# First layer's expert outputs kept as rows of a table that the second layer gathers, with half of each down weight split in two parts

## The chip, the cores and the metric

The kernel runs on one core of one Trainium2 chip. The metric is the device time of one execution in microseconds (us). Times named T+x are counted from one event of the profiled execution, which the text defines.

## What is computed

Two layers of a diffusion backbone over 512 latent tokens and 256 context tokens, width 1024, all float32. Each layer has an attention part and a mixture of experts; this is the mixture, cut to what matters here:

```python
# 16 experts in 4 groups; a token takes one group, and two experts inside it
for g in range(MOE_GROUPS):
    a = jnp.einsum('nd,edf->nef', h, w_gate[g])      # 1024 -> 256, per expert
    u = jnp.einsum('nd,edf->nef', h, w_up[g])        # 1024 -> 256
    hid = jax.nn.silu(a) * u * combine[:, g, :, None]   # zero but for the two chosen experts
    out = out + jnp.einsum('nef,efd->nd', hid, w_down[g])   # 256 -> 1024
...
x = x + mod_l[5] * f[:B * S].reshape(B, S, D)        # after layer 0: latent tokens
ctx = ctx + mod_c[5] * f[B * S:].reshape(ctx.shape)  # and context tokens
```

So a token's row after layer 0 is its row before, plus a gate row (one for latent, one for context tokens) times the sum of its two experts' outputs. Layer 1 norms that row first, and multiplies it with its input weights.

## The kernel before

Tokens stand in six tiles of 128 rows, taken in the order 4, 5 (context), 0, 1, 2, 3 (latent). Layer 0's output projection (`out_proj`) leaves the rows before the experts in DRAM as `F` and the normed rows as `H`, and the routing (`route_group`, `route`) gives each of the 16 experts up to 128 slots: `idx` holds the token of each slot.

**The expert loop** (`experts`, lines 1538 to 1594, called once per layer) runs over 16 experts, staggered: gate and up of expert e stand on TensorE ahead of down of expert e-1. Per expert:

- `fetch` (line 1026) gathers 128 rows of `H` through GpSimd's indirect DMA into `hg`; `expert_in` transposes them on TensorE and splits them in two float32r parts, `hh` on ScalarE and `hlo` on VectorE (`split`, lines 205 and 206).
- Weights come in units of 512 KB through `WeightStream`: four units with gate and up (two DMAs of 256 KB each), two with the down weight. 22 buffers hold them: the queue of SyncE issues a load when the buffer that it writes is free, in the order of use. Gate and up units are split in the parts `whi` and `wlo` as they come (`ahead`), at most four ahead (`nparts`), which frees the buffer; down units stay as they are until the matmuls have read them.
- `expert_up` (line 1043) multiplies in three terms of parts (hi hi, hi lo, lo hi), 24 matmuls of 512 columns into `eacc`. `expert_hid` transposes the hidden rows (`hidtr`) and copies them to `th`. `expert_down` (line 1079) does four plain float32 matmuls of 512 columns into two `yacc`; each stands in the profile as two instructions.
- `expert_gate` (line 1071) builds on VectorE the gate row of each slot (latent or context, by `ctx`), and `expert_down` multiplies `yacc` with it (line 1091) and adds the 128 rows to `F` by an indirect DMA with accumulation (line 1093), dropping empty slots:

```python
    nc.vector.tensor_tensor(y[:, cs], ya[n], gate[:, cs], op=ALU.mult)
i = nc.gpsimd.indirect_dma_start(F, bass.IndirectOffsetOnAxis(ap=idx[:, 1, x:x + 1], axis=0), y, None,
                                 compute_op=ALU.add, bounds_check=rows - 1, oob_is_err=False).ins
```

**The entry to layer 1** (in `emit`, lines 1633 to 1690) loads the six tiles of `F` (`xc`, three buffers, line 1665), and per tile `norm_hT` does: square and sum on ScalarE (line 779), reciprocal root on GpSimd (lines 211 and 212), scaling to `xn` on VectorE (line 781), eight transposes to `xtr` on TensorE, scale and shift to `tf` half on ScalarE and half on VectorE (lines 795 and 797), and the split into `hT` and `hL` (`hT1c` and `hL1c` for context tiles). Then TensorE multiplies with the key and value weights (`uk`, 256 columns) and, for latent tiles, with the first half of the query weights (`uq`, 512 columns, four units of two DMAs, loaded once the first `xc` has landed). TensorE's order in the expert loop is the program's (`manual_schedule`); at the entry the build's scheduler sets each engine's order. Every engine and queue works in order, so a waiting instruction holds what stands behind it.

## Time and profile before

| | us |
|---|---|
| median of 3 runs | 1223.6 (1219.67 to 1224.37) |
| the profiled execution | 1226.32, span 1224.6 |
| TensorE busy | 1105.9 (90%) |
| VectorE busy | 791.5 (65%) |
| ScalarE busy | 614.4 (50%) |
| GpSimd busy | 237.2 (19%) |

PE is TensorE's matmuls, PEld its weight loads, DVE VectorE, ACT ScalarE, POOL GpSimd, SP SyncE, and a name with q an engine's sequencer. A row of a timeline gives start, duration, engine, line, operation, output<-inputs, count, and in brackets how long the engine had been idle and what ended that. The expert loop of layer 0 lies at about 557 to 732 us, the entry to layer 1 at 732 to 800 us, the expert loop of layer 1 at 1043 to 1214 us.

### The profile page before, as it was taken

The numbers are of one execution on the slowest core, as the hardware profiler recorded it, in microseconds if no ns is written. First come the engines' busy times: TensorE is split into PE (matmuls) and PEld (weight loads), VectorE is DVE, ScalarE is ACT, GpSimd is POOL, SyncE is SP. The second block draws the span as 40 slices with busy tenths as digits, with TensorE's granted clock in tenths as the row PEclk, the third lists the DMA queues.
The fourth block names the chain that finished last, engine by engine and source line by source line (L and its number), as shares of the span: only waits on it lengthen the run. The fifth ranks groups of instructions, "written<-read, shape, count | busy, mean of one in ns | idle before, by whom it ended". The sixth has DMA issues, their size and how long they took to land.

```text
span 1224.6 us, 21495 instructions
## 1 busy us (share of the span) xinstructions
PE 1105.9 (90%) x7986; PEld 817.4 (67%) x7986; DVE 791.5 (65%) x1613; ACT 614.4 (50%) x1266; POOL 237.2 (19%) x252
## 2 busy tenths in 40 slices
PE   5999998998889989978999885989989996899996
PEld 2688887665556667866777654877766785677773
DVE  2532355677677753668888765677688447677773
ACT  3533644555466652216555536467588522555551
POOL 1000011224222000031222221331230004133321
PEclk8999999999899999978999996999999998899998
DMA  9711102776464428658999977012041374998992
GB/s 319 238 47 60 35 11 82 272 235 214 170 224 131 148 86 262 223 207 283 348 326 333 325 233 227 12 44 70 1 138 36 108 256 174 314 318 289 297 308 46
DMA packets 106251, 228.11 MB, mean 186 GB/s; under 512 B 21429, under 2 KB 30391, under 8 KB 106132
## 3 DMA queue, kind: packets, MB, share of 16 engines
q1 hardware_dynamic: 94324, 197.15, 48.0%
q0 software_dynamic: 9216, 22.09, 7.3%
q10 hardware_dynamic: 2592, 7.34, 1.5%
q8 instruction: 67, 1.10, 0.4%
q14 instruction: 52, 0.43, 0.1%
HBM read 210.60 MB, written 27.41 MB: 194 GB/s over the span
## 4 chain that ended last, share of the span: by engine, by line
PE 57%; DVE 8%; DMA 8%; ACT 4%; POOL 4%; issue 3%; SPq 1%; POOLq 0%; ACTq 0%; DVEq 0%
PE eacc L172 11%; PE acc L172 11%; PE yacc L172 7%; PE ptr L184 4%; DMA wraw<-in_exp_w_up_dram 4%; PE pv L172 4%; PE sc L172 4%; PE modps L172 3%; PE qacc L172 3%; PE hgtr L184 2%; PE co L172 2%; PE lg L172 2%; POOL rq L435 1%; DVE wlo L206 1%; PE h2tr L184 1%
## 5 line engine op out<-in xcount | busy, mean ns | idle before, releaser
L206 DVE TENSOR_TENSOR wlo<-wraw,whi 128x1024 fp32r<-128x1024 f32 (+2 forms) x184 | 210.2, 1156 | 80.9 <-ACT whi L205 71.0
L205 ACT CAST whi<-wraw 128x1024 fp32r<-128x1024 f32 (+2 forms) x184 | 181.1, 994 | 145.4 <-PE eacc L172 94.8
L172 PE MATMUL eacc<-whi,hh 128*128 128x512 f32 x256 | 119.7, 468 | 0.0
L172 PE MATMUL yacc<-wraw,th 128*128 128x512 f32 x256 | 115.2, 593 | 1.1 <-ACT th L1068 1.1
L172 PE MATMUL eacc<-whi,hlo 128*128 128x512 f32 x256 | 102.6, 401 | 0.0
L172 PE MATMUL eacc<-wlo,hh 128*128 128x512 f32 x256 | 102.2, 399 | 0.0
L172 PE MATMUL acc<-whi,hT 128*128 128x512 f32 (+2 forms) x256 | 91.8, 359 | 4.8 <-ACT hT L205 4.8
L172 PE MATMUL acc<-wlo,hT 128*128 128x512 f32 (+2 forms) x256 | 88.8, 347 | 0.5 <-DVE wlo L206 0.4
L184 PE MATMUL ptr<-cb,P 128*128 128x128 f32 x480 | 77.5, 284 | 12.8 <-ACT PT L540 6.4
L172 PE MATMUL acc<-whi,hL 128*128 128x512 f32 (+2 forms) x256 | 88.4, 345 | 0.0
L172 PEld LDWEIGHTS yacc<-wraw,th 128*128 128x128 f32 x256 | 48.2, 189 | 49.9 <-issue 44.1
L184 PEld LDWEIGHTS ptr<-cb,P 128*128 128x128 f32 x480 | 52.9, 141 | 38.8 <-ACT PT L540 9.9
L172 PE MATMUL modps<-mw,csT 128*32 128x512 f32 (+1 forms) x448 | 64.8, 571 | 10.4 <-DMA mw<-in_mod_w_dram 6.1
L172 PE MATMUL sc<-Kst,Qh 128*128 128x512 f32 (+2 forms) x192 | 64.7, 344 | 3.6 <-ACT P L544 3.5
L504 DVE CUSTOM_DVE_ANT_0 sc<-sc,mk,sink 128x512 f32<-128x512 f32 (+1 forms) x64 | 56.2, 882 | 16.8 <-PE sc L172 14.6
L540 ACT COPY PT<-ptr 128x512 f32<-128x512 f32 x96 | 56.1, 587 | 16.8 <-PE ptr L184 15.7
L172 PE MATMUL pv<-PT,z_k 128*64 128x256 f32 x480 | 63.7, 389 | 0.0
L172 PEld LDWEIGHTS eacc<-whi,hh 128*128 128x128 f32 x256 | 49.9, 195 | 14.5 <-issue 6.7
L172 PEld LDWEIGHTS eacc<-wlo,hh 128*128 128x128 f32 x256 | 50.0, 195 | 14.3 <-issue 6.7
L172 PEld LDWEIGHTS acc<-whi,hT 128*128 128x128 f32 x256 | 49.4, 193 | 14.5 <-ACT hT L205 5.2
L172 PE MATMUL sc<-Kst,Ql 128*128 128x512 f32 (+2 forms) x192 | 56.5, 316 | 1.1 <-DVE Ql L206 1.1
L172 PEld LDWEIGHTS eacc<-whi,hlo 128*128 128x128 f32 x256 | 49.3, 192 | 11.9 <-DVE hlo L206 0.7
(331 smaller groups left out, 2530.7 us busy)
## 6 DMA issues: line engine op xcount, KB each, us to landing
mw<-in_mod_w_dram SPq DMA_DIRECT2D x80, 512.0 KB
wraw<-in_exp_w_gate_dram SPq DMA_DIRECT2D x128, 256.0 KB
wraw<-in_exp_w_up_dram SPq DMA_DIRECT2D x128, 256.0 KB
wraw<-in_exp_w_down_dram SPq DMA_DIRECT2D x64, 512.0 KB
mw<-in_mod_w_dram SPq DMA_DIRECT2D x32, 256.0 KB
wraw<-in_ev_w_in_dram SPq DMA_DIRECT2D x12, 512.0 KB
wraw<-in_od_w_in_dram SPq DMA_DIRECT2D x20, 256.0 KB
wraw<-in_od_w_out_dram SPq DMA_DIRECT2D x16, 256.0 KB
```

The costliest lines, as they stand in the source:

```text
L172: return self.nc.tensor.matmul(out, lhsT=l, rhs=r, start=start, stop=stop)
L184: self.nc.tensor.transpose(out, in_, self.ident[:in_.shape[0], :in_.shape[0]])
L205: self.nc.scalar.copy(hi, src)
L206: self.nc.vector.tensor_tensor(lo, src, hi.bitcast(F32), op=ALU.subtract)
L435: nc.gpsimd.tensor_tensor(rq[:, 0, :], ms, self.mhalf[:, :8], op=ALU.pow)
L504: nc.vector.tensor_tensor_reduce(sc[:, lo:lo + L], sc[:, lo:lo + L], mask, rq[:, 1, h:h + 1], sink[:, 1, h:h + 1], ALU.add, ALU.min, mx[:, ...
L540: (nc.scalar.copy if a0 == 0 else nc.vector.tensor_copy)(u2["PT"][:, a0:a0 + m, j2, :], t[:, 0:m, :])
```

## The change

In layer 0 alone, an expert's output is no longer scaled and added to `F`: its 128 slots are copied from `yacc` (half by ScalarE, half by VectorE) and written as 128 rows of a DRAM table `Y` by a plain DMA from GpSimd's queue. The routing also computes for each token its two rows of the table (`slot`; one more row holds zeros, for a pair that got no slot). At the entry to layer 1, two indirect DMAs per tile gather these rows (`fetch_y`, two tiles ahead), and VectorE adds the two, multiplies with the gate row and adds to `xc`; latent tiles are written back to `F`. In layer 0 the first of the two down units of each expert is split in parts too, with one more unit ahead (`nparts` and the parts' buffers 5 in place of 4), and multiplies in three terms. Layer 1's expert loop stays.

```diff
-                    self.units.append((False, [(slice(0, 2), wd[...])]))
+                    self.units.append((l == 0 and q == 0, [(slice(0, 2), wd[...])]))
...
+            V.tensor_tensor(by, r["OH"], self.cst("iota")[:, None, None, 0:16].to_broadcast([P, 2, T, 16]), op=ALU.mult)
+            V.tensor_reduce(sl, by, axis=AX.X, op=ALU.add)
+            V.scalar_tensor_tensor(sl, sl, float(P), r["pos"], op0=ALU.mult, op1=ALU.add)
+            V.tensor_scalar(far, r["pos"], float(CAP), float(2 * NEXP * P), op0=ALU.is_ge, op1=ALU.mult)
+            V.tensor_tensor(sl, sl, far, op=ALU.add)
+            V.tensor_scalar(self.slot, sl, float(NEXP * P), None, op0=ALU.min)
...
-    def expert_gate(self, e, gate, isctx, wk):
-        y = wk.tile([P, D], F32, tag="y", name="y", bufs=2)
-        self.nc.vector.scalar_tensor_tensor(y, gate[1], isctx[:, e:e + 1], gate[0], op0=ALU.mult, op1=ALU.add)
...
+        hi, lo = [wk.tile([P, P], F32R, tag=n, name=n, bufs=2) for n in ("thh", "thl")]
+        self.split(hi, lo, t[:, 0, :])
+        self.nc.scalar.copy(th[:, 1, :], t[:, 1, :])
...
             for n in range(2):
-                self.mm(ya[n], h[:, q, :], w[:, n, :], q == 0, q == 1)
+                if not isinstance(w, tuple):
+                    self.mm(ya[n], (h[0] if isinstance(h, tuple) else h)[:, q, :], w[:, n, :], q == 0, q == 1)
+                    continue
+                for c, (a, b) in enumerate(((1, 0), (1, 1), (2, 0))):
+                    self.mm(ya[n], h[a], w[b][:, n, :], c == 0, False)
+        if gate is None:
+            for n in range(2):
+                (nc.scalar.copy, nc.vector.tensor_copy)[n](y[:, n * 512:(n + 1) * 512], ya[n])
+            nc.gpsimd.dma_start(self.Y[x * P:(x + 1) * P, :], y)
+            return
...
+        def fetch_y(t):
+            yi[t] = [spare(oh, 2 * (t % 2) + j) for j in range(2)]
+            return [nc.gpsimd.indirect_dma_start(yi[t][j], None, k.Y, bass.IndirectOffsetOnAxis(ap=k.slot[:, j, t:t + 1], axis=0)).ins
+                    for j in range(2)]
...
-            d = nc.sync.dma_start(xi[i], F[i * P:(i + 1) * P, :]).ins
+            ds = [nc.sync.dma_start(xi[i], F[i * P:(i + 1) * P, :]).ins]
+            if m not in g5:
+                g5[m] = spare(ol, m)
+                nc.sync.dma_start(g5[m], k.modD[0][m, 5 * D:6 * D].partition_broadcast(P))
+            if t < 2:
+                ds += fetch_y(t)
             if first is None:
-                first = d
+                first = ds[2]
...
+                ya, yb = yi[t]
+                nc.vector.tensor_tensor(ya, ya, yb, op=ALU.add)
+                nc.vector.tensor_tensor(ya, ya, g5[m], op=ALU.mult)
+                nc.vector.tensor_tensor(xi[i], xi[i], ya, op=ALU.add)
+                if t + 2 < 6:
+                    fetch_y(t + 2)
                 k.norm_hT(wk, pt, xi[i], AB1[:, m, :], k.modT[1][:, m, 0:8], *parts(i))
+                if i < 4:
+                    nc.scalar.dma_start(F[i * P:(i + 1) * P, :], xi[i])
```

Three places show what this does to the order of instructions. Each fence lists one engine's instructions in order (line, operation, output<-inputs, columns, count if repeated).

**TensorE, where down of one expert stands in layer 0's loop.** Before:

```order
L172 MATMUL eacc<-wlo,hh 128x512
L172 MATMUL eacc<-whi,hlo 128x512
L172 MATMUL yacc<-wraw,th 128x512 x4
L172 MATMUL eacc<-whi,hh 128x512
L172 MATMUL eacc<-wlo,hh 128x512
```

Now:

```order
L175 MATMUL eacc<-whi,hlo 128x512
L175 MATMUL yacc<-whi,thh 128x512
L175 MATMUL yacc<-wlo,thh 128x512
L175 MATMUL yacc<-whi,thl 128x512
L175 MATMUL yacc<-whi,thh 128x512
L175 MATMUL yacc<-wlo,thh 128x512
L175 MATMUL yacc<-whi,thl 128x512
L175 MATMUL yacc<-wraw,th 128x512 x2
L175 MATMUL eacc<-whi,hh 128x512
```

Two of the four float32 matmuls are now three matmuls of parts each; nothing else moved there.

**VectorE and ScalarE at the entry to layer 1, first tiles** (`wlo` and `whi` here are parts of the query weights `uq`). VectorE before:

```order
L781 TENSOR_SCALAR xn<-xc,ss 128x1024 x2
L797 TENSOR_SCALAR tf<-xtr,AB_4100,modT_70 128x128 x4
L781 TENSOR_SCALAR xn<-xc,ss 128x1024
L206 TENSOR_TENSOR hL1c<-tf,hT1c 128x4x128 x2
L781 TENSOR_SCALAR xn<-xc,ss 128x1024
L797 TENSOR_SCALAR tf<-xtr,AB_4100,modT_70 128x128 x2
L206 TENSOR_TENSOR wlo<-wraw,whi 128x1024
```

VectorE now, the first three rows and the next three being the adds of the first and the second tile:

```order
L1715 TENSOR_TENSOR early_oh_8053<-early_oh_8053 128x1024
L1716 TENSOR_TENSOR early_oh_8053<-early_oh_8053,early_ol_8054 128x1024
L1717 TENSOR_TENSOR xc<-xc,early_oh_8053 128x1024
L1715 TENSOR_TENSOR early_oh_8053<-early_oh_8053 128x1024
L1716 TENSOR_TENSOR early_oh_8053<-early_oh_8053,early_ol_8054 128x1024
L1717 TENSOR_TENSOR xc<-xc,early_oh_8053 128x1024
L209 TENSOR_TENSOR wlo<-wraw,whi 128x1024 x2
L786 TENSOR_SCALAR xn<-xc,ss 128x1024
L209 TENSOR_TENSOR wlo<-wraw,whi 128x1024 x2
L802 TENSOR_SCALAR tf<-xtr,AB_4102,modT_70 128x128 x4
L209 TENSOR_TENSOR hL1c<-tf,hT1c 128x4x128
```

ScalarE before:

```order
L779 ACTIVATE xn,ss<-xc 128x1024 x2
L795 ACTIVATE tf<-xtr,modT_70,AB_4100 128x128 x4
L779 ACTIVATE xn,ss<-xc 128x1024
L205 CAST hT1c<-tf 128x4x128 x2
L779 ACTIVATE xn,ss<-xc 128x1024
```

ScalarE now:

```order
L784 ACTIVATE xn,ss<-xc 128x1024
L208 CAST whi<-wraw 128x1024 x2
L784 ACTIVATE xn,ss<-xc 128x1024
L208 CAST whi<-wraw 128x1024 x2
L800 ACTIVATE tf<-xtr,modT_70,AB_4102 128x128 x4
L208 CAST hT1c<-tf 128x4x128 x2
```

The six adds and all four splits of `uq` now stand ahead of the first tile's `tf` on VectorE, and the four casts of `uq` ahead of it on ScalarE; before, the first split of `uq` stood behind the first tile.

**VectorE and GpSimd, between the first tile and the third one's `xn`** (the third tile, 0, is the first latent one). VectorE now, from the row behind the second tile's `xn` on:

```order
L209 TENSOR_TENSOR hL1c<-tf,hT1c 128x4x128
L1715 TENSOR_TENSOR early_oh_8053<-early_oh_8053 128x1024
L802 TENSOR_SCALAR tf<-xtr,AB_4102,modT_70 128x128 x4
L209 TENSOR_TENSOR hL1c<-tf,hT1c 128x4x128
L1716 TENSOR_TENSOR early_oh_8053<-early_oh_8053,early_ol_8054 128x1024
L209 TENSOR_TENSOR hL1c<-tf,hT1c 128x4x128
L1717 TENSOR_TENSOR xc<-xc,early_oh_8053 128x1024
L1715 TENSOR_TENSOR early_oh_8053<-early_oh_8053 128x1024
L405 TENSOR_REDUCE ms<-ktmp 128x2
L1716 TENSOR_TENSOR early_oh_8053<-early_oh_8053,early_ol_8054 128x1024
L1717 TENSOR_TENSOR xc<-xc,early_oh_8053 128x1024
L786 TENSOR_SCALAR xn<-xc,ss 128x1024
```

GpSimd now, around the reciprocal root (`ss`) of that third tile:

```order
L1688 DMA early_oh_8053<-Y,slot 128x1024 x2
L214 TENSOR_SCALAR ss<-ss 128x1
L1688 DMA early_oh_8053<-Y,slot 128x1024
L215 TENSOR_TENSOR ss<-ss,mhalf 128x1
L214 TENSOR_SCALAR ms<-ms 128x2
```

Before, the third tile's `xn` followed the first tile's `tf` directly, and no DMA stood in GpSimd's queue here. Now six adds (of the third and the fourth tile) stand between, and a gather for the sixth tile stands inside the root's pair; that gather needs the buffer that the fourth tile's adds read.

## Rows read from the trace of the kernel before

**Rows 1.** Busy time by stretch: stretch, its us, busy us and instructions, TensorE clock, DMA share, GB/s.

```profile
630.00:660.00 30.00, 30.00 (x127) 21.15 (x126) 25.89 (x30) 17.16 (x24) 7.87 (x6) 1.00 1.01 340
...
731.00:742.00 11.00, 0.00 (x0) 0.00 (x0) 0.57 (x1) 0.31 (x2) 1.56 (x1) 0.69 0.57 134
...
750.00:763.00 13.00, 10.26 (x66) 8.76 (x64) 10.51 (x19) 11.26 (x22) 3.09 (x6) 0.89 0.83 272
763.00:800.00 37.00, 37.00 (x217) 32.18 (x217) 24.68 (x60) 19.48 (x48) 12.52 (x18) 0.96 0.07 19
```

**Rows 2.** The chain that ended last: start us, us, what held it.

```profile
552.38 4.49 DMA hg<-H,idx
...
604.84 2.74 PE eacc L172 x12
607.58 3.43 PE yacc L172 x8
...
617.69 3.43 PE yacc L172 x8
...
688.24 10.28 DMA wraw<-in_exp_w_up_dram
...
703.43 3.43 PE yacc L172 x8
...
731.84 6.33 DMA F<-y,idx
738.25 3.43 DMA xc<-F
```

**Rows 3.** Timeline of ScalarE in layer 0's expert loop.

```profile
675.37 1.04 ACT L205 CAST whi<-wraw 128x1024 fp32r<-128x1024 f32 x1 [6.01 <-DMA wraw<-in_exp_w_up_dram]
```

**Rows 4.** DMA, 552 to 558 us, gathers alone: packets, MB, share of 16 engines.

```profile
q0 software_dynamic: 273, 1.01, 56.4%
```

**Rows 5.** DMA, 731 to 738 us, the last accumulation alone.

```profile
q0 software_dynamic: 272, 0.64, 56.1%
```

**Rows 6.** DMA, 597 to 698 us, by queue, and two kinds of issue.

```profile
q1 hardware_dynamic: 11663, 25.43, 68.6%
q0 software_dynamic: 2877, 7.84, 30.4%
...
F<-y,idx POOLq DMA_INDIRECT x10, 9.1
hg<-H,idx POOLq DMA_INDIRECT x9
```

**Rows 7.** Groups by line and shape, 571 to 735 us: count, busy us, mean ns.

```profile
L206 DVE TENSOR_TENSOR wlo<-wraw,whi 128x1024 fp32r<-128x1024 f32 x57 | 68.5, 1220 | 25.1 <-ACT whi L205 18.8 <-issue 4.1 <-DMA wraw<-in_exp_w_down_dram 0.8
L205 ACT CAST whi<-wraw 128x1024 fp32r<-128x1024 f32 x56 | 58.7, 1049 | 63.8 <-PE eacc L172 40.1 <-DMA wraw<-in_exp_w_up_dram 20.3 <-issue 2.4
...
L1091 DVE TENSOR_TENSOR y<-yacc,y 128x512 f32<-128x512 f32 x32 | 20.8, 681 | 1.6 <-PE yacc L172 1.4
L1076 DVE SCALAR_TENSOR_TENSOR y<-g,ctx,g 128x1024 f32<-128x1024 f32 x16 | 20.4, 1278 | 0.0
```

**Rows 8.** One line's instructions, `h<-h,B`: durations in ns, minimum, median, maximum.

```profile
L882 DVE TENSOR_TENSOR h<-h,B x6: 1212/1224/1226, 504.7 to 1022.7; 128x1024 f32<-128x1024 f32 x6
```

**Rows 9.** Timeline, from the last expert of layer 0 into layer 1.

```profile
730.88 0.69 DVE L1091 TENSOR_TENSOR y<-yacc,y 128x512 f32<-128x512 f32 x1 [0.17 <-PE yacc L172]
...
741.70 1.06 ACT L779 ACTIVATE xn<-xc 128x1024 f32<-128x1024 f32 x1 [10.69 <-DMA xc<-F]
...
744.02 0.75 DVE L781 TENSOR_SCALAR xn<-xc,ss 128x1024 f32<-128x1024 f32 x1
...
748.13 1.36 DVE L797 TENSOR_SCALAR tf<-xtr,AB,modT 128x128 f32<-128x128 f32 x4
...
750.59 0.56 PE L172 MATMUL acc<-whi,hT1c 128*128 128x256 f32 x1
...
751.03 12.92 SPq L317 DMA_DIRECT2D wraw<-in_od_w_in_dram  x11
```

66 lines of the change are left out of this document (39 added, 27 removed).

## The prediction

> **What bounds the kernel now.** I read the busy time by stretch first. In layer 0's expert loop TensorE is busy 30.00 of 30 us and the DMA engines are full at the same time (share 1.01, 340 GB/s); from 731 to 742 TensorE does nothing, and from 763 to 800 it is busy 37.00 of 37 us [rows 1]. So there are two places to look at: a loop with two limits, and an entry to layer 1 whose length is set by when TensorE gets its third tile, since after that it never waits.
>
> Next comes the chain that ended last. One expert takes 617.69 - 607.58 = 10.11 us, of which down (`yacc`) is 3.43 us, or 0.43 for each of its eight instructions, and twelve `eacc` take 2.74 us, 0.229 each [rows 2]. Late in the loop the chain leaves TensorE and runs through loads of weights, one of which lands 10.28 us after its issue, at 698.52 [rows 2]; the timeline shows ScalarE idle for 6.01 us until a weight has landed [rows 3]. From 607.58 to 703.43 nine experts took 95.85 us, 4.9 more than nine times 10.11 [rows 2]: that is what the loads cost the loop.
>
> At its end the last accumulation into `F` takes 6.33 us to land, then the first `xc` 3.43 [rows 2]. I count from T = 730.88 + 0.69 = 731.57, when VectorE has written the last output [rows 9]. Before, the first tile's square starts at 741.70 = T+10.1, its first product at 750.59 = T+19.0 [rows 9], and TensorE's unbroken work with the third tile at 763 = T+31.4 [rows 1].
>
> **TensorE in the loop.** Two of four float32 matmuls (four instructions of 0.43 = 1.72 us) become six matmuls of parts (6 x 0.229 = 1.37) [rows 2]: 0.34 us less per expert, 5.5 for sixteen, as long as nothing else sets the pace. VectorE gets one split more (1.22) and a small one, and one copy in place of two products (2 x 0.68), and loses the gate row (1.28) [rows 7]; its load of 25.89 in 30 us [rows 1] does not rise. ScalarE gets a cast (1.05) [rows 7], two small copies and one of 512 columns on top of 17.16 in 30 [rows 1], about 2.3 us per expert, and stays under 8 of 10 us. Both are covered by TensorE; without that cover the gain of 0.34 would be gone.
>
> **DMA in the loop.** Gathers alone: 1.01 MB took 56.4% of 6 us, 3.35 us of all engines per MB [rows 4]. An accumulation alone: 0.64 MB took 56.1% of 7 us, 6.1 us per MB [rows 5], 1.8 times as much. In the full stretch, 101 us, ten accumulations and nine gathers together, 7.84 MB or 0.41 MB each, took 30.4%, 30.7 us [rows 6]; with the ratio of 1.8 that is 2.77 us per MB gathered and 5.0 accumulated. An accumulation then costs 2.05 us of all engines, and a table write of the full 128 rows (0.52 MB) at the plain price 1.45: 0.6 less. I take the plain price because the write only reads SBUF and writes DRAM; the other end is that of an accumulation, no gain. Eleven such writes lie ahead of the landing at 698.52, so it comes 6.6 us earlier. Behind it, three experts are each 0.34 shorter, and one small wait for a load (0.3, an estimate) goes: **7.9 us less in the loop**. The lower end, with loads no cheaper, is the last three downs and that wait, 1.3. The upper end is all of 5.5 + 4.9 = 10.4, when TensorE alone sets the pace. The added zero row, the slots' six small operations and the two gate rows no longer loaded lie beside the routing's and the first gather's waits (4.49 us [rows 2]); I cost them at nothing, 0.5 either way.
>
> **The entry, first step.** The table write is seen nowhere in the trace. Its landing lies between a plain load of its size, 3.43, and an accumulation, 6.33 [rows 2]; nearest is the gather of 128 rows, which GpSimd issues too, 4.49 [rows 2], and I take 4.0, between it and the load. GpSimd starts 731.84 - 731.57 = 0.27 after T [rows 2, 9]. Then the gathers of one tile: 4.49, plus 1.1 for the second, a third of the 3.4 us that three gathers kept the engines [rows 4]. They are there at T+9.9. Three operations of 1024 columns on VectorE follow, 1.22 each like the nearest row [rows 8]: the first square at T+13.5, 3.4 later than before. Lower end 0.6 less, upper end 2.3 more.
>
> **The entry, second step: VectorE's queue.** The order shows what VectorE must do between those gathers and the product of the third tile, which before had none of the adds ahead of it. Counted to the half tile that TensorE needs: 14 of the adds' operations (14 x 1.22 = 17.1), four splits of `uq` (4 x 1.22 = 4.9), four `xn` (3.0), three times `tf` (3 x 1.36 = 4.1), five `hL` of 512 columns (half of 1.22 each, 3.1), and five small ones of the keys (1.6, an estimate) [rows 7 to 9]. The sum is 33.8 us, so the third tile's product starts at T+43.7 if VectorE never waits: 12.3 later than T+31.4. It will wait twice. The first tile's `tf` now stands behind all of `uq` on ScalarE and VectorE, and `uq` is loaded only once the first gathers have landed, behind two `xc`. Eleven such loads took SyncE 12.92 us [rows 9], so the eight take 9.4, and with the `xc` ahead (2.6, an estimate from 3.43 each, overlapped) the last is split at about T+23; by then VectorE has had some 10.5 us of work since T+9.9, 2 to 3 us less than there is time. And the third tile's root stands on GpSimd behind a gather that waits for the fourth tile's adds, about 1 us. Together some 3.5: the product at T+47.2. What goes with the old order is the wait for the accumulation; what is late next is VectorE. Since TensorE's 37 us behind this point are unbroken [rows 1] and the same, the shift goes through to the end: **15.8 us more at the entry**, between 11 (VectorE never waits, and the write lands early) and 18 (the write lands like an accumulation). The last two tiles' four remaining operations fit into VectorE's 24.68 of 37 us there [rows 1], and the write-back of `F` is read long after.
>
> A page weighs against the trace here. The gather that I price by took 4.49 us [rows 2]. The Trainium skill, in "DMA: Bandwidth & Descriptors", section "Anatomy of one DMA — SWDGE (gpsimd) path", fits a GpSimd-issued DMA as 2.0 us plus its bytes at 436 GB/s. By that fit, an estimate, write and first gathers would come 1.7 us earlier than I take, and the sum would be 1229.8. The trace's gather is slower than the fit's 3.2, so I keep the row.
>
> **The sum.** -7.9 + 15.8 = +7.9 us. On the profiled execution (1226.32) that makes 1234.2; it was 2.7 above the median of the runs, so I set the sum on the median: 1223.6 + 7.9 = 1231.5, with 1227 to 1237 as this case's own range. A measurement of this kernel can tell about 0.5%, 6.1 us, from no change: 1217.5 to 1229.7.
>
> **The rivals.**
> - *Both at their good ends* (0.26): the loop gains 10.4 because the loads no longer hold it, and VectorE's queue costs its sum without waits, 11 to 12.3. That is about +1.5, 1225. For it: the loop's loads were late by only 4.9 us in all. Against: the four splits stand where VectorE must wait.
> - *Faster* (0.17): the entry costs only the first step. TensorE's third tile comes when its own chain allows, T+31.4 + 3.4, because the adds fall into VectorE's gaps: it was busy 10.51 of 13 us there [rows 1]. With 10.4 from the loop the time is 1223.6 + 3.4 - 10.4 = 1216.6. It decides by whether the third tile's product starts before about T+37. Against it: six adds alone are 7.3 us ahead of the first tile, and the gaps of that stretch are 2.5.
> - *Slower still* (0.15): a table write of 128 rows costs the engines what an accumulation of some 100 rows does, the loads stay as late, and the loop gives back 1.3 only. With 15.8 to 18 at the entry: 1238 to 1240.
>
> My forecast keeps 0.42. Faster by more than 0.5%: 0.17. Slower by more: forecast 0.38 (0.04 of it falls below 1229.7) and the last rival's 0.15, 0.53. Within: 0.26 + 0.04 = 0.30. The range 1218 to 1240 leaves out most of the faster rival and the end of the slower one, some 0.2.
>
> **What would show it.** In the new profile: down as six instructions at 0.229 and four at 0.43; a pace of 9.8 us per expert early in the loop; ScalarE's wait for a load shorter than 6 us or later; GpSimd's table writes landing in about 4 us at the end. At the entry: the first adds near T+9.9, `tf` of the first tile behind the last cast of `uq`, VectorE full from there to the third tile, and TensorE's third tile near T+47 with no wait behind it. I am wrong if that tile starts before T+37, if TensorE waits again between it and the attention, or if the loop is not shorter by 5 to 10 us.

## The result and the profile after

The changed kernel takes 1253.05 us (median of 4 runs, 1251.13 to 1253.83), the kernel before 1222.52 in runs beside it: a ratio of 1.0239, 95% interval 1.0219 to 1.0258 (the two medians alone give 1.0250). It is slower, as forecast, but by about 29 us and not by 8: it lies 13 us above the top of the range. The profiled execution took 1253.83, its span is 1252.1, 27.5 more than before's 1224.6.

The same point T, the end of VectorE's last output, is now 733.39 + 0.69 = 734.08, where 731.57 was: 2.5 us later, where 7.9 earlier was forecast. The loop began at another time too. This is TensorE's first product with the first expert's weights, in the kernel before and in the changed one:

```profile
558.70 0.80 PE L172 MATMUL eacc<-whi,hh 128*128 128x512 f32 x1
```

```profile
556.65 0.80 PE L175 MATMUL eacc<-whi,hh 128*128 128x512 f32 x1
```

From there to T the loop takes 177.4 us, before 172.9. So it is 4.6 longer, of which a start 2.1 earlier hides a part. That start is scatter: over the runs below it lies between 551.5 and 559.9, also in kernels with the same code up to there.

From T to TensorE's third tile it was 31.3 us and is 790.86 - 734.08 = 56.8, so the entry costs 25.5 more, not 15.8. Behind that tile the span has 461.2 us left, before 461.7. So the loop and the entry hold the whole result; each has a cause of its own.

**The loop.** Busy time by stretch of the changed kernel, columns as in [rows 1]:

```profile
630.00:660.00 30.00, 27.29 (x122) 20.36 (x121) 23.07 (x28) 19.62 (x31) 7.08 (x6) 1.00 1.03 378
697.00:734.00 37.00, 34.13 (x141) 24.12 (x139) 24.72 (x33) 23.09 (x38) 2.20 (x4) 1.00 0.47 158
734.00:746.00 12.00, 0.00 (x0) 0.00 (x0) 2.76 (x9) 1.43 (x2) 2.51 (x3) 0.59 0.52 181
746.00:760.00 14.00, 0.00 (x0) 0.00 (x0) 7.00 (x6) 2.19 (x3) 6.83 (x6) 0.50 0.91 327
760.00:791.00 31.00, 14.90 (x77) 13.53 (x77) 25.26 (x39) 15.59 (x31) 13.91 (x16) 0.61 0.71 241
791.00:828.00 37.00, 36.86 (x215) 32.11 (x215) 26.59 (x57) 18.86 (x46) 12.90 (x18) 0.96 0.12 43
```

From 630 to 660 TensorE is busy 27.29 of 30 us, where it was 30.00: it waits. The DMA engines move 378 GB/s, where they moved 340, at a share of 1.03 (before 1.01), and from 697 on they are half idle (0.47). The loads come in time, and still the loop is longer. The chain that ended last (start, us, what) gives the pace in the loop, and behind it the first steps of the entry:

```profile
605.96 2.77 PE eacc L175 x12
608.72 2.98 PE yacc L175 x10
...
616.85 2.76 PE eacc L175 x12
619.60 2.98 PE yacc L175 x10
...
734.60 4.14 DMA Y<-yo
740.81 5.42 DMA early_oh<-Y,slot
746.31 1.24 DVE early_oh L1715
749.75 12.09 DMA wraw<-in_od_w_in_dram
```

Down is ten instructions in 2.98 us in place of 3.43 [rows 2], as forecast (3.09). But one expert takes 616.85 - 605.96 = 10.89 us and not 9.8. What TensorE waits for, 577 to 735 us (instruction, what it waited for, us in total, times, longest), in the changed kernel:

```profile
PE hgtr L187 <- ACT th L1086: 11.7, 13, 0.9
```

and in the kernel before:

```profile
PE hgtr L184 <- ACT th L1068: 3.1, 2, 1.9
```

`hgtr` is the transpose of the gathered rows into PSUM, `th` ScalarE's copy of the hidden rows out of PSUM. The timeline of one expert, columns as in [rows 9]:

```profile
613.03 0.38 PE L187 MATMUL hidtr<-cb,sg 128*128 128x128 f32 x2
...
614.23 0.26 ACT L208 CAST thh<-hidtr 128x128 fp32r<-128x128 f32 x1
614.36 1.22 DVE L209 TENSOR_TENSOR wlo<-wraw,whi 128x1024 fp32r<-128x1024 f32 x1 [1.11 <-ACT whi L208]
...
615.50 0.28 DVE L209 TENSOR_TENSOR thl<-hidtr,thh 128x128 fp32r<-128x128 f32 x1
615.82 0.27 ACT L1086 COPY th<-hidtr 128x128 f32<-128x128 f32 x1 [1.33 <-DVE thl L209]
...
616.13 0.71 PE L187 MATMUL hgtr<-cb,hg 128*128 128x128 f32 x4 [0.91 <-ACT th L1086]
```

Read it from the bottom. `hgtr` needs a buffer in PSUM, where this kernel's matmuls and transposes write; the two buffers of its tag (`tr`) are shared with `hidtr`. The one it needs is `hidtr`'s, which is free when its last reader is done. Before, that was one copy on ScalarE. Now it is three steps on two engines: ScalarE's cast `thh`, VectorE's `thl`, then ScalarE's copy `th`, which waits 1.33 us for `thl`. And `thl` stands in VectorE's queue behind a split of weights (`wlo`, 1.22). TensorE stops for 0.91 us, once per expert.

**The DMA engines.** Queues from 597 to 698 us (packets, MB, share of 16 engines) and the median landing of the table writes:

```profile
q1 hardware_dynamic: 13367, 29.73, 80.1%
q0 software_dynamic: 2753, 8.70, 21.7%
...
Y<-yo POOLq DMA_DIRECT2D x9, 512.0 KB, 7.4
```

GpSimd's queue now moves 8.70 MB in 21.7% of 101 us, 2.5 us per MB, against 30.7 us for 7.84 MB, 3.9 per MB [rows 6]. Weights get 29.73 MB where they got 25.43. Of ScalarE's waits for weights in the loop, 20.3 us before [rows 7], one of 0.32 us is left (571 to 735 us).

**The entry.** From the timeline of the changed kernel, all engines, from the first gathers to TensorE's third tile:

```profile
746.31 1.22 DVE L1715 TENSOR_TENSOR early_oh<-early_oh 128x1024 f32<-128x1024 f32 x1 [9.55 <-DMA early_oh<-Y,slot]
...
746.49 1.86 POOL L1688 DMA_INDIRECT early_oh<-Y,slot  x1 [4.71 <-DMA early_oh<-Y,slot]
...
750.09 1.06 ACT L784 ACTIVATE xn<-xc 128x1024 f32<-128x1024 f32 x1 [14.55 <-DVE xc L1717]
...
755.68 1.04 ACT L208 CAST whi<-wraw 128x1024 fp32r<-128x1024 f32 x1 [4.44 <-DMA wraw<-in_od_w_in_dram]
...
756.60 1.23 DVE L1715 TENSOR_TENSOR early_oh<-early_oh 128x1024 f32<-128x1024 f32 x1 [6.55 <-DMA early_oh<-Y,slot]
...
760.47 1.04 ACT L208 CAST whi<-wraw 128x1024 fp32r<-128x1024 f32 x1 [3.75 <-DMA wraw<-in_od_w_in_dram]
...
790.86 0.56 PE L175 MATMUL acc<-whi,hT 128*128 128x256 f32 x1
```

The table write took 4.14 us to land, as forecast (4.0). The first gathers are there at 746.3, T+12.2. GpSimd then issues the second tile's gathers, at 746.49, because the program makes them wait for the first's landing; their rows come at 756.6, T+22.5, and VectorE has idled 6.55 us for them. The loads of `uq` are also released by the first gathers, and ScalarE waits for them twice, 4.44 and 3.75.

### The profile page after: what moved, and what is told of

It is laid out like the page before. It is cut to its first block, busy times and chain, and to the rows that moved or that the text cites. A ratio compares the mean times of both kernels' runs of the same rounds, so it can differ in the third digit from the quotient of the medians.

```text
span 1252.1 us, 21738 instructions
## 1 busy us (share of the span) xinstructions
PE 1102.3 (88%) x8018; PEld 822.8 (66%) x8018; DVE 809.5 (65%) x1634; ACT 641.1 (51%) x1314; POOL 244.6 (20%) x266
## 3 DMA queue, kind: packets, MB, share of 16 engines
q1 hardware_dynamic: 94324, 197.15, 46.9%
## 4 chain that ended last, share of the span: by engine, by line
PE 57%; DVE 10%; issue 5%; ACT 5%; POOL 4%; DMA 3%; SPq 0%; DVEq 0%; POOLq 0%; ACTq 0%
PE acc L175 11%; PE eacc L175 11%; PE yacc L175 8%; PE ptr L187 4%; PE pv L175 4%; PE sc L175 4%; PE modps L175 3%; PE qacc L175 3%; PE hgtr L187 2%; ACT whi L208 2%; PE co L175 2%; DVE wlo L209 2%; PE lg L175 1%; POOL rq L440 1%; DMA wraw<-in_od_w_in_dram 1%
## 5 line engine op out<-in xcount | busy, mean ns | idle before, releaser
L209 DVE TENSOR_TENSOR wlo<-wraw,whi 128x1024 fp32r<-128x1024 f32 (+2 forms) x200 | 230.7, 1162 | 91.9 <-ACT whi L208 81.6
L208 ACT CAST whi<-wraw 128x1024 fp32r<-128x1024 f32 (+2 forms) x200 | 197.8, 999 | 119.1 <-PE eacc L175 65.4
L187 PE MATMUL ptr<-cb,P 128*128 128x128 f32 x480 | 77.6, 284 | 12.2 <-ACT PT L545 5.7
L175 PE MATMUL yacc<-wraw,th 128*128 128x512 f32 x192 | 87.6, 592 | 0.5 <-ACT th L1082 0.5
L187 PE MATMUL hgtr<-cb,hg 128*128 128x128 f32 x256 | 39.6, 290 | 22.7 <-ACT th L1086 11.7
L175 PEld LDWEIGHTS yacc<-wraw,th 128*128 128x128 f32 x192 | 36.2, 189 | 33.9 <-issue 29.5
L175 PE MATMUL sc<-Kst,Ql 128*128 128x512 f32 (+2 forms) x192 | 56.3, 315 | 1.1 <-DVE Ql L209 1.1
```

The lines of the kernel that those rows point to most:

```text
L175: return self.nc.tensor.matmul(out, lhsT=l, rhs=r, start=start, stop=stop)
L187: self.nc.tensor.transpose(out, in_, self.ident[:in_.shape[0], :in_.shape[0]])
L208: self.nc.scalar.copy(hi, src)
L209: self.nc.vector.tensor_tensor(lo, src, hi.bitcast(F32), op=ALU.subtract)
```

## The experiments

Where no other unit stands, times are us, and T is each kernel's own. Ratios are to the kernel before as it ran beside each, with 95% intervals; they are those on record, and the quotient of the two medians can be 0.002 off them. The loop is counted from the first expert's first product to T.

| kernel | median (runs) | ratio | T | loop | third tile |
|---|---|---|---|---|---|
| before | 1222.5 to 1225.1 | 1 | 731.57 | 172.9 | T+31.3 |
| the change | 1253.05 (4) | 1.0239 [1.0219, 1.0258] | 734.08 | 177.4 | T+56.8 |
| e1_parts | 1235.64 (5) | 1.0078 [1.0040, 1.0115] | 739.67 | 183.9 | T+32.0 |
| e2_table | 1244.12 (4) | 1.0142 [1.0106, 1.0179] | 727.52 | 167.6 | T+56.4 |
| e3_whole | 1240.16 (4) | 1.0118 [1.0082, 1.0153] | 720.91 | 164.2 | T+56.3 |
| e4_uq | 1247.41 (4) | 1.0164 [1.0125, 1.0203] | 737.29 | 178.9 | T+50.7 |
| e5_noadds | 1242.05 (2) | 1.0151 [1.0119, 1.0183] | 732.45 | 177.4 | T+46.9 |
| e6_prefetch | 1228.50 (10) | 1.0044 [1.0029, 1.0059] | 718.02 | 164.1 | T+44.2 |
| e7_l1 | 1219.41 (12) | 0.9971 [0.9955, 0.9987] | 730.59 | 175.0 | T+31.9 |
| e8_hybrid | 1236.89 (5) | 1.0108 [1.0091, 1.0125] | 719.26 | 162.7 | T+56.3 |
| e9_pref | 1230.19 (6) | 1.0054 [1.0023, 1.0085] | 732.46 | 174.4 | T+37.8 |
| e10_both | 1227.84 (6) | 1.0033 [0.9998, 1.0068] | 731.90 | 173.9 | T+37.4 |
| e11_pref_noadds | 1229.76 (2) | 1.0051 [0.9994, 1.0108] | 719.09 | 162.6 | T+48.4 |
| e12_root | 1232.09 (6) | 1.0067 [1.0043, 1.0091] | 718.82 | 164.2 | T+44.0 |
| e13_all | 1229.13 (10) | 1.0045 [1.0029, 1.0061] | 715.71 | 164.2 | T+43.3 |
| e14_l1 | 1225.92 (12) | 1.0028 [1.0010, 1.0045] | 720.84 | 164.2 | T+42.4 |
| e15_nogather | 1228.17 (10) | 1.0018 [0.9987, 1.0048] | 719.91 | 164.2 | T+44.4 |
| e16_parts_whole | 1223.40 (10) | 0.9980 [0.9951, 1.0008] | 728.15 | 173.8 | T+31.6 |
| e17_nodep | 1250.01 (4) | 1.0203 [1.0167, 1.0238] | 735.11 | 179.3 | T+50.0 |
| e18_best | 1222.05 (12) | 0.9989 [0.9969, 1.0008] | 721.58 | 164.2 | T+41.0 |

The last three columns come from one profile of each kernel, and they tell where a large difference lies. Small ones may be scatter. Kernels with the same loop code give 172.9 to 175.0 (before, e7, e9, e10), 177.4 to 179.3 (the change, e4, e5, e17) and 162.6 to 164.2 (e3, e6, e11 to e15, e18) for the loop, and 454 to 465 us follow the third tile's product.

### The two halves of the change, each alone: e1 and e2

e1 is the kernel before with the parts of the down weight in layer 0, no table; e2 is the change with the down weight left whole:

```diff
-                    self.units.append((l == 0 and q == 0, [(slice(0, 2), wd[...])]))
+                    self.units.append((False, [(slice(0, 2), wd[...])]))
...
-            st.nparts = 5 - l
+            st.nparts = 4
```

> The kernel before with half of down in parts and nothing of the table. Theory (in the profile of the change TensorE waits 0.9 us in 13 experts, 11.7 in all, for ScalarE's second copy of the hidden rows: the second half of hgtr needs the PSUM buffer that hidtr holds until that copy, which stands behind VectorE's thl): the wait is here too, about 13 times 0.9, the loop runs at 10.9 us per expert, its last output comes at about 734 against 731.6 before, the entry is as before: 1224 to 1227 us. Rival (the copies of yacc to the table rows hold ScalarE up, and the split alone does not): no such wait, 1218 to 1222.

> The change without down in parts: table, gathers and adds only. Theory: no wait at hgtr, a pace of 10.07 to 10.11 us per expert throughout because the table writes hold the engines less than accumulations did, last output at about 727 (4.9 earlier than before); entry 25 us longer as in the change: 1241 to 1245 us. Rival (the table writes do not relieve the loads): last output at 731 to 732, 1246 to 1249.

In e1 the loop is 11.0 longer than before, and the wait is there without any table (what TensorE waited for, 577 to 730 us):

```profile
PE hgtr L187 <- ACT th L1076: 16.3, 13, 1.3
```

The mechanism is the expected one; its size is not, for T was expected at 734 and the time at 1224 to 1227. VectorE, which still builds the gate rows here, is busy 106.83 of 120 us from 577 to 697 (92.11 in the change), and the longest wait is 1.3 in place of 0.9.

In e2, which has the table and no parts, this wait does not occur, TensorE is busy 120.00 of 120 us from 577 to 697, and the loop is 5.3 shorter than before. The entry is the change's own (T+56.4 against T+56.8), while e1's is that of before (T+32.0). So the parts lose in the loop, and the table gains in the loop and loses at the entry.

### The PSUM buffer given back by one copy: e3

```diff
+        self.nc.scalar.copy(th, t[:, 0:2, :])
         if not two:
-            self.nc.scalar.copy(th, t[:, 0:2, :])
             return th
...
-        self.split(hi, lo, t[:, 0, :])
-        self.nc.scalar.copy(th[:, 1, :], t[:, 1, :])
+        self.split(hi, lo, th[:, 0, :])
```

> The change, but the hidden rows are copied out of PSUM whole in one copy as before, and the parts are made from that copy. Theory of the PSUM buffer: TensorE's wait at hgtr goes, pace about 9.75 us per expert, last output near 722.5 in place of 734.1, entry unchanged: 1240 to 1243 us. Rival (ScalarE's and VectorE's queues of splits, or five buffers of parts, set the pace): pace 10.4 or more, 1248 to 1253.

ScalarE copies the hidden rows out of PSUM in one piece, as before, and the parts are made from the copy in SBUF. Busy time of e3, 577 to 697 us, and two steps of its chain:

```profile
577.00:697.00 120.00, 120.00 (x543) 91.77 (x541) 103.38 (x126) 93.18 (x137) 26.92 (x23) 1.00 1.02 385
```

```profile
606.88 3.08 PE yacc L175 x10
...
616.58 3.08 PE yacc L175 x10
```

TensorE is full again, at 9.70 us per expert, and the loop is 13.2 shorter than in the change. VectorE and ScalarE have the same splits and the same five buffers of parts, are busier than in the change (103.38 and 93.18 us against 92.11 and 80.74) and are still covered. The wait was the whole of the loop's loss: without it the loop is 8.7 shorter than before (8.7 to 10.7 over the four profiles of that loop), and 7.9 was forecast.

### Query weights behind the first rows: e4

```diff
-                first = ds[2]
+                first, row = ds[2], ds[0]
...
-        uq = k.proj_units(..., 512, after=first)
+        uq = k.proj_units(..., 512, after=row)
```

> The change, but the loads of the query weights and of the later rows stand behind the first load of rows of F, as before the change, and no longer behind the first tile's gathers. Theory (the splits of the query weights hold ScalarE and VectorE ahead of the first tile's tf because their loads come late, and take the engines from the second tile's gathers): the casts no longer wait, the first tile's transposes start 6 to 9 us earlier than the 29.5 us after the last output that they start now, and the third tile's product comes 5 to 8 earlier: 1245 to 1248 us. Rival (VectorE's work and the gathers alone set the third tile): at most 2 us gained, 1251 to 1253.

The loads now follow the first `xc` and not the first gathers. They run beside the table write and the gathers, which get slower: the first rows land at 754.66, T+17.4 in place of T+12.2, and the first transposes start at T+32.8 (T+29.5 in the change). The third tile still comes 6.1 earlier. So the wait for the gathers had kept the loads off the table write and the first gathers: without it the first tile comes later and the third earlier.

### Adds: e5

e5 leaves out the sum of the two rows and the product with the gate row (two of the three operations on VectorE in each tile).

> The change without the first two of the three adds of each tile: one gathered row is added to the row of F, the other row and the gate row are left out (the output is not the reference's). Theory (behind the first tile VectorE's adds set the third tile): eight operations of 1.23 us are gone ahead of it, the first tile still waits for the query weights, and the third tile's product comes 6 to 10 us earlier: 1243 to 1247 us. Rival (the gathers and the query weights set it, the adds lie in their waits): 1250 to 1253.

The third tile comes 9.9 earlier. In the change ten such operations of 1.22 us stand ahead of it, 12.2 us. But the first add, which now needs one of the two gathers only, also starts 2.8 earlier (T+9.4), so 7.1 are left for the work of 12.2: it counts, and not in full, because a part of it comes back as waits (VectorE waits 9.01 for the second tile's rows and 5.70 for a split of `uq`). 15.6 of the entry's 25.5 us remain without it.

### Weights in time: e6, and its counterpart without the table: e9

e6 is e3 with the loads of `uq` issued ahead of the first `xc` and waiting for no gather: two of its four units go into space that is not yet in use, the other two through the stream's buffers. e9 does this in the kernel before, with all four units in space of their own.

```diff
         xi = {}
+        uq = k.proj_units(..., raws=[ol[:, 2 + h, :].rearrange(...) for h in range(2)])
...
-        uq = k.proj_units(hl, ..., 512, after=first)
```

> The run with the hidden rows copied whole, and the query weights loaded ahead of the end of the loop: their loads wait for no rows and stand ahead of them in SyncE's queue, two of the four units in a spare part of the gathers' buffer. Theory (the engines of the DMAs are idle in the last 20 us of the loop, and the casts wait only for the loads): casts and splits lie in the 12 us in which ScalarE and VectorE wait for the first gathers, the first tile's transposes start near 20 us after the last output in place of 29.5, the third tile's product near 43 to 47 in place of 56.8: 1226 to 1231 us. Rival (VectorE's adds and the gathers set it): not below 1235.

> The kernel before, with nothing of the change, and the query weights loaded ahead of the end of layer 0's loop, into a buffer that lies free until the attention. Theory (in the kernel before, too, the third tile waits for these weights: the chain runs from a load at 748.61 through two splits to the product at 763.16): the third tile's product comes 3 to 8 us earlier than 31.4 us after the last output, 1217 to 1221 us. Rival (the rows of F and VectorE set it): within 1 us of before.

In e6 the third tile comes 12.1 earlier than in e3 (T+44.2), and the time falls by 11.7. The loads are not free there: the first adds start at T+15.6 (e3 T+12.5), and the first transposes stay at T+29.5, where about T+20 was expected.

e9 is a miss: the third tile comes 6.5 later than before (T+37.8). The chain of e9 shows when the first rows are even issued:

```profile
746.24 3.62 DMA xc<-F
```

That is T+13.8; before it was 738.25, T+6.7 [rows 2]. Two things hold this load, in about equal parts. The last accumulation into `F`, issued at 732.74, has the early loads beside it and lands after 9.9 us in place of 6.33 [rows 2]. Then, from 742.6 on, SyncE itself is late. It reaches the branch behind the loop (line 1105) at 736.0, when it has issued the eight early loads (729.74 to 735.98), and its instructions there end at 746.1; before it was there from 718.3 to 724.4. ScalarE, which has the early weights to cast, waits for the same:

```profile
745.81 1.28 ACT L205 ACT_TABLE_LOAD   x1 [17.83 <-SPq L1105]
```

So the same kind of edit gains 12.1 in one kernel and loses 6.5 in the other. Idler DMA engines are not the difference: in the 21 us ahead of T their share is 0.64 in e3 and 0.73 in the kernel before. What differs is what stands behind: in e3 all splits of `uq` stand ahead of the first tile's `tf`, in the kernel before they do not, and there the first rows wait for the accumulation and for SyncE. No run takes these apart.

### Accumulation for the last experts: e8

Twelve experts write the table, whose rows are gathered and added ahead of the loop's end; the last four accumulate into `F` as before.

```diff
-        if gate is None:
+        if l == 0 and e < 12:
             for n in range(2):
...
+    for t in range(3):
+        fetch_y(t)
```

> The run with the hidden rows copied whole, but only the first 12 experts write table rows; the last four are scaled and accumulated into F as before. The table rows of three tiles are gathered, summed and scaled without waiting for the rows of F, and one add per tile is left behind them. Theory (the loads are relieved where it matters, and the entry waits for an accumulation and a load as before, with one add of 1.23 us per tile behind them): last output 8 to 11 us earlier than before, entry 3 to 8 longer: 1216 to 1222 us. Rival (the sums still stand ahead of the third tile on VectorE): entry 12 or more longer, 1224 or more.

A miss. The gathers of the table's rows run beside the last accumulation, which takes 10.11 us to land in place of 6.33 [rows 2], as e8's chain has it:

```profile
720.99 10.11 DMA F<-y,idx
...
731.18 6.44 DMA xc<-F
```

That is 3.8 of the 25.0 by which the entry is longer than before, and the first `xc` adds 3.0 (3.43 before [rows 2]). Further on the chain has a load of `uq` (8.37) and a gather (7.34); how much of the rest is theirs is not shown.

### What holds the rest of the entry: e11, e12, e13, e15

e11 is e6 without the two operations that e5 leaves out. e12 is e6 with the later gathers behind the previous tile's root on GpSimd, and the second tile's adds behind the first tile's `xn` on VectorE. e13 is e12 with all four units of `uq` in space of their own, and the next weights behind the first gathers. e15 is e6 without the gathers of the last four tiles; its adds stay, on what lies in their buffers. The core of e12's edit, with e13's:

```diff
-                if t + 2 < 6:
-                    fetch_y(t + 2)
                 k.norm_hT(wk, pt, xi[i], ...)
+                if t + 2 < 6:
+                    for d in fetch_y(t + 2):
+                        k.after(d, k.root)
...
-                          raws=[ol[:, 2 + h, :]...])
+                          raws=[ol[:, 2 + h, :]...] + [zq[0][:, 2 * h:2 * h + 2, :] for h in range(2)])
```

> The run with the query weights loaded early on the change, without the first two of the three adds of each tile (one gathered row and the gate row are left out of the result). Theory (with the weights out of the way VectorE's adds set the third tile, and only the write, the gathers and one add are left): 8 to 12 us less than that run's 1228.5: 1216 to 1221 us. Rival (the gathers' landing sets the third tile): at most 4 less.

> The run with the query weights loaded early on the change (1228.5), with a tile's later gathers put behind the root of the tile before on GpSimd, and the second tile's adds behind the first tile's scaling on VectorE. In that run the first tile's root waits on GpSimd behind a gather that waits for VectorE, which waits for the second tile's rows. Theory (this queue costs the first tile 6 us): its transposes start 22 to 23.5 us after the last output in place of 29.5, the third tile's product 39 to 43 in place of 44.2: 1223.5 to 1227.5 us. Rival (VectorE's work sets the third tile whatever stands first): 1228 to 1230.

> As the run beside it, but all four units of query weights go to free buffers, so that none is left to load while the last table row is written, and the next weights wait for the first gathers. Theory (in the run with early weights the last write landed 6.3 us after its issue because six loads ran beside it, in place of 4.1 in the change): the write lands near 4.7 us after the last output again, everything behind it 2 us earlier: 1221 to 1226 us. Rival (the write's time is not on the path): as the run beside it.

> The run with the query weights loaded early on the change (1228.5), without the gathers of the last four tiles: their adds stay and take what the first two tiles' buffers hold (so the rows of the table are left out of four tiles). Theory (with the weights out of the way the third tile waits for its gathers, which start only when the first tile's adds have freed the buffer, and the adds lie in that wait): the third tile's product near 36 to 39 us after the last output in place of 44.2, 1221 to 1224 us. Rival (VectorE's adds set it): no earlier than 43, 1227 to 1230.

e12 brings the first transposes 7 us forward, as expected (T+22.4, e6 T+29.5), and the third tile not at all (T+44.0), as its rival had it. e13's first adds come 2.1 earlier, as expected (T+13.5), and its third tile at T+43.3; e15's missing gathers leave it at T+44.4. In e6, e12, e13 and e15 the first add of the second tile starts at T+24.4, T+24.6, T+22.9 and T+24.9, and the third tile's product follows 19.5 to 20.4 later, whatever else was moved. e11 says nothing: in its VectorE queue the fourth tile's add, waiting 4.28 us for its `xc`, stood ahead of the first tile's last parts.

### The second tile's gathers let go: e17

```diff
             else:
-                for d in ds:
-                    k.after(d, first)
+                k.after(ds[0], first)
```

> The change, but only the first of the loads behind the first gathers waits for them; the second tile's two gathers and the loads behind may start at once. My theory: part of the entry's miss is that the second tile's rows land at T+22.5 and not with the first's near T+12; without the wait they land at about T+15, VectorE's idle 9.55 and 6.55 us there shrink, but the loads of the query weights still hold the first tile's half to about T+27, so the third tile's product comes at T+50 to 56 and the time is 1246 to 1253. Rival: what the engines of the DMA move in that time is what counts, and gathers and loads only trade places: third tile at T+56 to 58, 1252 to 1255.

From the timeline of e17, GpSimd's issues of the first tile's second gather and the second tile's first, and VectorE's first adds of each tile:

```profile
741.85 0.97 POOL L1688 DMA_INDIRECT early_oh<-Y,slot  x1 [0.30 <-issue]
743.12 0.94 POOL L1688 DMA_INDIRECT early_oh<-Y,slot  x1 [0.30 <-issue]
...
747.18 1.23 DVE L1714 TENSOR_TENSOR early_oh<-early_oh 128x1024 f32<-128x1024 f32 x1 [9.39 <-DMA early_oh<-Y,slot]
...
750.84 1.22 DVE L1714 TENSOR_TENSOR early_oh<-early_oh 128x1024 f32<-128x1024 f32 x1
```

The second tile's adds follow the first's without a gap, at T+15.7 in place of T+22.5, and the third tile moves by the same 6.8 us, from T+56.8 to T+50.0. The loads of `uq` did not come earlier: the last split ends at T+35.6, later than the change's T+31.8. The wait was the program's own, and it was on the path. Its size is less clear, for the scheduler's order changed with the edit: from the first add to the third tile's product VectorE waits 9.5 us in place of 12.4 and works 28.5 in place of 32.1.

### Versions meant to win: e7, e10, e14, e16, e18

e16 puts e3's way of making parts into layer 0 of the kernel before, without a table; e7 does it in layer 1 instead, and takes two of that layer's weight buffers away to make room for the parts (`NY`: 22 in place of 24; layer 0 has 17, not 22 as said above). e10 is e7 with e9's early loads, e14 is e13 with e7's parts in layer 1, and e18 is e14 with e17's edit. e7's edit, against the kernel before:

```diff
-                    self.units.append((False, [(slice(0, 2), wd[...])]))
+                    self.units.append((l == 1 and q == 0, [(slice(0, 2), wd[...])]))
...
         self.nc.scalar.copy(th, t[:, 0:2, :])
-        return th
+        if not two:
+            return th
+        hi, lo = [wk.tile([P, P], F32R, tag=n, name=n, bufs=2) for n in ("thh", "thl")]
+        self.split(hi, lo, th[:, 0, :])
+        return th, hi, lo
...
-NX, NY = (7, 15), (10, 9)
+NX, NY = (7, 15), (10, 7)
```

> The kernel before, layer 0 untouched, with half of down in parts in layer 1 instead, hidden rows copied whole, two weight buffers fewer to make room. Theory: layer 1's loop is bound by TensorE (busy 30 of 30 us from 1073 to 1193, DMA share 0.90 to 0.97), so 0.34 us per expert shows: 4 to 5.5 us less than before, a pace of 9.75 us. Rival (the loads cannot follow that pace): TensorE waits for casts late in that loop, at most 2 us less.

> The run with half of down in parts in layer 1, and the query weights loaded early as in the run beside it. The two act in different places, so their gains add: 1212 to 1216 us; if the early loads gain nothing, 1219 to 1220 as that run alone.

> As the run with all four units loaded early, with half of down in parts in layer 1 too (two weight buffers fewer there). The gain in layer 1 was 4 to 5 us on the kernel before, and should be the same here: 4 to 5.5 us less than the run beside it, 1216 to 1222 us, faster than the kernel before.

> The kernel before with half of down in parts in layer 0, the hidden rows copied whole, and nothing of the table. Theory (without the table the loads of that loop set its pace): no wait at hgtr, but waits for loads as before, last output within 1.5 us of the 731.6 of before, 1222 to 1226 us. Rival (TensorE sets the pace): a pace of 9.75 us, last output 3 to 5 us earlier, 1218 to 1221.

> The kernel with all pieces together (early query weights, later gathers behind the root, parts in layer 1) and with the second tile's gathers not waiting for the first's. Theory: the third tile's product comes about 20 us after the second tile's rows have landed (T+23 to 25 in three kernels, product at T+42 to 44); with the rows at T+15 to 17 it comes at T+36 to 39, and the time is 1217 to 1222. Rival: VectorE's work from the first gathers on sets it, whenever the second tile's rows land; then T+42 or more, and 1224 to 1228.

e7 is the only kernel that is measurably faster than the one before: 0.9971, interval 0.9955 to 0.9987, about 3.5 us. Layer 1's loop had TensorE busy 120.00 of 120 us at a DMA share of 0.93 (1073 to 1193 us), so less work for TensorE pays there until loads become late. The chain of e7 in that loop:

```profile
1129.60 3.08 PE yacc L175 x10
1139.30 3.08 PE yacc L175 x10
1149.42 10.49 DMA wraw<-in_exp_w_gate_dram
1159.97 13.76 DMA wraw<-in_exp_w_gate_dram
1173.80 7.50 DMA wraw<-in_exp_w_down_dram
```

The pace is 9.70 us (10.08 before), until loads of weights take over the chain at 1149.42 and a part of the gain is given back. Whether the DMA engines (share 0.92 from 1073 to 1193 us) or the two buffers fewer make these loads late is not shown. e10 adds e9's loss to e7 (third tile at T+37.4) and misses its 1212 to 1216 by far. e14 is 3.2 below e13, less than the 4 to 5.5 expected, and not faster than the kernel before.

e16's loop takes 173.8, no less than the 172.9 to 175.0 of the kernels with before's loop; its T is 3.4 earlier because the loop starts earlier. There loads still hold the loop (ScalarE waits 15.6 us for up weights, 577 to 730 us), and its 0.9980 can't be told from no change. So in layer 0 the parts gain nothing by themselves; with the table's lighter traffic they gain 3.4 (e2's loop 167.6, e3's 164.2). e7 and e16 together were not run.

e18 reaches T+41.0, between the two expectations, and with it 0.9989: the table with every repair tried here, and with layer 1's parts, is no slower than the kernel before, and no faster. e7, which has layer 1's parts without the table, stands at 0.9971. In e18 T is 10.0 earlier than before (the loop 8.7 shorter), the third tile comes 9.7 later from there, and the gain of layer 1's parts is not told apart from the spread.

## Why the prediction was right and wrong

- **Direction: right.** The loop was to gain less than the entry loses; e3, whose loop gains as forecast, shows it (1240.16, ratio 1.0118). The rival "faster" needed the third tile before T+37; it came at T+56.8, so VectorE's gaps did not take the adds. "Slower still" named too little gain in the loop, but for another reason: the table write did not cost what an accumulation does.
- **TensorE's and the DMA engines' terms in the loop: right.** Down 2.98 to 3.09 us (3.09 forecast), the table's traffic at 2.5 us per MB (2.77 forecast for gathers and plain writes), the loads no longer late. e3 shows what these are worth together: a loop 8.7 us shorter, near the 7.9 forecast. The table alone gives 5.3 of it (e2; 6.6 forecast).
- **The step that failed in the loop: "Both are covered by TensorE"**, said of ScalarE's and VectorE's added work. Their loads are covered (VectorE 23.07, ScalarE 19.62 of 30 us), but the forecast added up busy times and did not ask which buffer that work holds. The new split reads `hidtr` in PSUM on both engines, one after the other, and TensorE's next transposes need that buffer: 0.9 us per expert, 11.7 in 13 experts, and 13.2 in the whole loop (e3). So the loop is 4.6 us longer and not 7.9 shorter, which the forecast itself named as a sign of being wrong. At T this is 10.4 us of the 21.6 by which the forecast missed (2.5 in place of -7.9); it would be 12.5 if the loop had not started 2.1 earlier. The code of `expert_hid` stood in the diff, with `t[:, 0, :]` as the source of the split; the trace of before showed this very wait twice, 3.1 us.
- **The entry's first step: nearly right.** The write landed in 4.14 (4.0 forecast). The Trainium skill, in "DMA: Bandwidth & Descriptors", section "Anatomy of one DMA — SWDGE (gpsimd) path", fits 2.0 us plus the bytes at 436 GB/s, which is 3.2 us for this write, an estimate; the trace's 4.14 decides against it. The forecast's "1.7 us earlier" by that fit is 2.1 from its own numbers (4.0 and 4.49 against 3.2 each), also an estimate, and nothing else hangs on it. The gathers were there at T+12.2, not T+9.9, and the first square started at T+16.0, not T+13.5: the write's issue at T+0.5 and not T+0.27, 0.76 us between the write's landing and GpSimd's first issue (738.74 and 739.50) and an issue of 1.00 for the first gather, and 5.42 us to land for the second. "Upper end 2.3 more" was passed, by 0.2 at the square.
- **The step that failed at the entry: "so the third tile's product starts at T+43.7 if VectorE never waits", and the 3.5 us allowed for two waits.** The 33.8 us of VectorE's work were right: it is busy 32.12 of the 44.55 us from its first add to the third tile. But it waits 12.4 us there. So the sum was forecast as 9.9 + 33.8 + 3.5 = 47.2 and is 12.2 + 32.1 + 12.4 = 56.8 (rounded): the waits are most of the miss. The largest is 6.55 us for the second tile's rows, for which the forecast had no wait. The program's order makes those gathers wait for the first's landing, and they take another 10.1 us from issue to adds. e17 takes this wait away and the third tile moves by 6.8 us, of the 9.6 missed; how much of that is the wait alone, and how much the order that changed with it, is not shown.
- **The loads of `uq`: the mechanism right, the size off.** Their last split ends at T+31.8, not T+23, and in e6 early weights alone bring 12.1 us, although the first adds start 3.1 later for them. The two gains overlap: e17 brings 6.8, e6 12.1, and e18, which has both and more, 15.8. Each wait hides a part of the other, so neither number may be added to the other.
- **The root behind a gather on GpSimd: right, and not decisive.** The first tile's root shows it (a gather waits 5.69 us for VectorE's first add inside the pair); e12 takes it away and gains nothing at the third tile. At the third tile's own root, which the forecast priced at about 1 us, VectorE waits 1.55.
- **The rest: right.** TensorE's 37 us behind the third tile are all but unbroken (36.86 of 37), and the shift went through to the end. The profiled execution lies 0.8 above its median, where before's lay 2.7 above; this gives 1.9 of the miss.

What stays open: why the third tile still needs 19.5 to 20.4 us from the second tile's adds in e6, e12, e13 and e15, and 21.3 in e18. Counted from the first tile's first add it is 28.0 to 29.9 us in e6, e12 to e15 and e18, and VectorE is busy 20.9 to 22.8 of them. In e18 its largest gaps are 2.61 us for rows and 2.20 for a root, and TensorE's granted clock there is 0.60; no run took VectorE's work, these gaps and the clock apart, since e11's order spoiled that test.

## What to carry to other kernels

Before work is called covered because the other engine is busier, ask for each new instruction which buffer it reads last and who waits for that buffer; here a split that two engines made from PSUM in turn held the buffer through both queues, and one plain copy first gave it back. When work is moved from a busy loop to a serial stretch, write down every transfer there with what releases it, one tile after the other, and don't let a sum of busy times start from the first tile's landing as if all rows were there. An early load is not free: ask which transfer on the path runs beside it and what its queue has to do behind it. The same kind of edit gained 12 us behind the table's loop and lost 6 in the kernel before, where an accumulation on the path and SyncE's next load came later for it. And before a shift of 2 or 3 us at one point of a profile is called a gain, see where the stretch began: e16's 3.4 us at T were an earlier start.

## What the runs showed that was not expected

- At a full DMA share, the rate depends on what is moved: 378 GB/s with table writes and gathers, 340 with accumulations and gathers, at shares of 1.03 and 1.01. Table and parts alone separate it: 379 in e2, 343 in e1 (577 to 697 us, shares 1.02 and 1.01). GpSimd's queue fell from 3.9 to 2.5 us per MB.
- A transfer on the path stretches beside others: the last accumulation took 6.33 us to land alone [rows 2], 10.11 beside gathers of the table's rows (e8) and 9.9 beside early loads (e9).
- TensorE's granted clock is 0.50 from 746 to 760 us in the change, where it has no work: the lower of its two levels, 1.2 GHz. The first tile's products then follow each other at 0.21 us (768.60, 768.82), and from 773.80 on at 0.12 (773.80, 773.92). Before, it is the same for a shorter time: 0.21 at first (751.67, 751.88), 0.11 from 752.26 on (752.26, 752.37), and the clock is 0.89 from 750 to 763 [rows 1]. So 6.5 us of the first products run at the lower clock in the change, 1.7 before. What that costs the third tile is not shown.
